# A bidirectional SSD layer: scan outputs and branch sums taken in PSUM instead of from two SBUF operands

## The chip, the cores and the metric

One core of a Trainium2 chip runs the whole layer. The metric is the device time of one execution in microseconds (us); a run of the kernel gives one number, and the median of several runs is compared. For this kernel 0.2% is about 2.6 us.

## The reference

One layer of a hybrid encoder on a sequence of 512 tokens with 1,024 features, all in 32-bit floats. What matters here is the state-space branch of the mixer:

- `h = RMSNorm(x)`, then one projection gives `z`, the scan inputs (after a short convolution and SiLU: `xs`, `B`, `C`) and two step sizes per head, `dt_fwd` and `dt_bwd`.
- 32 heads of 64 features are in 4 groups of 8 heads. Each head is scanned forward and backward in chunks of 128 tokens. In each direction the output of a token is `y_diag` (from its own chunk) plus `y_off = (C . state that enters the chunk) * exp(a_cum)`, where `a_cum` is the running sum of `dt * A` within the chunk.
- `y = y_fwd + y_bwd + d_skip * xs`, then `y * SiLU(z)` is normalised over each group of 512 features, and the normalised `y` is projected by `w_branch_ssd` (2,048 to 1,024).

Then come a windowed attention branch, a gated merge with an output projection, cross-attention into a memory of 256 tokens, a SwiGLU feed-forward part and a last RMSNorm.

## The kernel before, in words

Activations lie with features on the 128 partitions and the 512 tokens along the free dimension. Each weight is split into a high and a low half in a reduced-precision matmul format, and so is each activation; a product is three matmuls (L140 to L142), so that TensorE has 3 matmuls of 128x512 per weight block. Weights are read in pieces of 128x1024 by SyncE; ScalarE makes the high half (L130), VectorE the low half (L131).

The eight PSUM banks are three pools: three banks `mm` for projections, two `sa`, three `sb`. A bank is free for its next matmul when its last reader is done.

The scan stage runs from about 100 to 530 us. For each of the 4 groups the steps of `group_in` (projection and convolution of `B`, `C`, `xs`), `group_z` (the gate), `group_scan` and `group_out` are lists of closures which `weave` merges. Group g's `group_out` is merged into the scan of group g+1, and the last one stands alone behind the scans.

- `group_scan`, per head: SyncE loads a row of `a_cum`, spread over the partitions, into `rt` (L519); GpSimd masks it (`affine_select`, L538), ScalarE takes exponentials (L545), GpSimd adds the two directions into `mt` (L551), VectorE multiplies by `C.B` (L556), TensorE multiplies with `xs` into a bank `sa` (L566).
- Per pair of heads, `arrive` (L572) makes the arriving part of both directions in two `sb` banks, `yo[i,0]` and `yo[i,1]` (L578), and `gather` (L582) puts the output together: L586 makes `vv = xs * d_skip + yd`; L590 multiplies the loaded exponentials `ear` by `yo` and writes the product over `ear` in SBUF; L591 adds this to `vv`, on VectorE for the forward and on GpSimd for the backward direction. The forward part has tokens 128 to 511, the backward part tokens 0 to 383.
- `gate` (L595) multiplies `vv` by the gate (L603), splits it (L192, L193) and adds its square into `sq_acc` (L188).
- `group_out` (L637): eight accumulations of 12 matmuls in `mm` banks. For group 0, L645 writes `acc * vrow` into `bs`. For groups 1 to 3, L648 (VectorE) writes `acc * vrow` into the SBUF tile `cvt`, of which there is one, and L649 (GpSimd) adds it to `bs`. `vrow` is the row of norm factors. The convolution (L416 to L418) uses the same tile `cvt`.
- `apply_early` (L664) multiplies four blocks of `bs` by the merge gate once the last `group_out` has filled them.

What each engine does in which order is not written by hand alone: the kernel runs in two blocks opened with `schedule_with_timeline_sim=True` (L1136), in which a planner takes the program order as priority and a model of durations, and writes the order of each engine. The first block ends at about 530 us. At run time each engine takes its instructions strictly in that order.

Of the kernel before, what the change touches and what calls it, by code (L numbers as in the profile page):

```python
# [9 lines left out]
F32 = mybir.dt.float32  # L10
F32R = mybir.dt.float32r
AF = mybir.ActivationFunctionType
ALU = mybir.AluOpType
AX = mybir.AxisListType

P = 128
D = 1024
S = 512
# [55 lines left out]
def bidir_hybrid_layer(ctx: ExitStack, tc: tile.TileContext, io, dbg=None):  # L74
    nc = tc.nc
# [12 lines left out]
    bs = x1  # L88
# [6 lines left out]
    def bank(tag):  # L95
        return ps.tile([P, 512], F32, tag=tag, name=tag, bufs={"mm": 3, "sa": 2, "sb": 3}[tag])
# [16 lines left out]
    def gcol(c):  # L113
        return vec[:, c:c + 1]
# [20 lines left out]
    def mac(acc, w, xh, xl, nk=KT, k0=0, w0=0, first=True, last=True):  # L135
        hi, lo = w
        for k in range(nk):
            wh = hi[:, (w0 + k) * P:(w0 + k + 1) * P]
            wl = lo[:, (w0 + k) * P:(w0 + k + 1) * P]
            nc.tensor.matmul(acc, wh, xh[:, k0 + k], start=first and k == 0, stop=False)  # L140
            nc.tensor.matmul(acc, wh, xl[:, k0 + k], start=False, stop=False)  # L141
            nc.tensor.matmul(acc, wl, xh[:, k0 + k], start=False, stop=last and k == nk - 1)  # L142
# [55 lines left out]
    st = {}  # L198
# [5 lines left out]
    def full(src):  # L204
        return (src, 1024)
# [284 lines left out]
    def group_scan(g):  # L490
# [91 lines left out]
        def gather(i):  # L582
            def f():
                st["vv", i] = vv = st["sp"].tile([P, S], F32, tag="vv", name="vv", bufs=2)
                ear = st["ear", i]
                nc.vector.scalar_tensor_tensor(vv, st["xs", g, i], gcol(V_DSK + 4 * g + i), st["yd", i],  # L586
                                               op0=ALU.mult, op1=ALU.add)
                for d, eng in ((0, nc.vector), (1, nc.gpsimd)):
                    t = slice(P, S) if d == 0 else slice(0, S - P)
                    nc.vector.tensor_tensor(ear[:, d, t], ear[:, d, t], st["yo", i, d][:, t], op=ALU.mult)  # L590
                    eng.tensor_tensor(vv[:, t], vv[:, t], ear[:, d, t], op=ALU.add)  # L591
            return f


# [20 lines left out]
        for t in range(HPG + LAG3 + 1):  # L615
# [3 lines left out]
            if t >= LAG3 and (t - LAG3) % 2 == 0 and t < HPG + LAG3:  # L619
                i = (t - LAG3) // 2  # L620
                order += [nn[i], ar[i]]
            if t >= LAG3 + GLAG and (t - LAG3 - GLAG) % 2 == 0:
                i = (t - LAG3 - GLAG) // 2
# [13 lines left out]
    def group_out(g):  # L637
        def f2(q):
            def f(w):
                for j in range(2):  # L640
                    m = 2 * q + j
                    acc = bank("mm")
                    mac(acc, w, st["vh"], st["vl"], nk=4, w0=4 * j)
                    if g == 0:
                        nc.vector.tensor_tensor(bs[:, m], acc, st["vrow"], op=ALU.mult)  # L645
                    else:
                        t = st["sp"].tile([P, S], F32, tag="cvt", name="cvt", bufs=1)
                        nc.vector.tensor_tensor(t, acc, st["vrow"], op=ALU.mult)  # L648
                        nc.gpsimd.tensor_tensor(bs[:, m], bs[:, m], t, op=ALU.add)  # L649
            return f  # L650
        return [(f2(q), (full(io["w_bs"][g, q]),)) for q in range(4)]

# [589 lines left out]
```

## Time and profile before

| | |
|---|---|
| median of 3 runs | 1304.64 us (1303.63 to 1304.96) |
| the profiled execution: its time | 1304.59 us |
| the profiled execution: its span, first to last instruction | 1302.8 us |
| TensorE busy | 1253.3 us (96%) |
| VectorE, ScalarE, GpSimd busy | 770.9, 565.7, 314.8 us (59%, 43%, 24%) |
| mean granted TensorE clock | 0.989 |

How to read it: the time of an execution is its span and 1.8 us around it. PE is TensorE's matmul, PEld its weight load, DVE VectorE, ACT ScalarE, POOL GpSimd, SP SyncE. A row of the timeline has its start, its duration, and in brackets the idle time of the engine just before it with what ended that idle time. Consecutive instructions of one kind are merged (x2), and their rows can overlap by some 0.1 us, since an engine begins an instruction while the one before is still writing.

### The profile page before, as it was taken

To read this page: it belongs to the slowest core of one execution; us is meant where nothing else is said; L and a number is where in the kernel's file an instruction comes from. 1 tells how busy PE (TensorE), PEld (TensorE's weight loads), DVE (VectorE), ACT (ScalarE), POOL (GpSimd) and SP (SyncE) were. 2 spreads that over 40 slices of the span, in tenths; PEclk is the share of its full clock that TensorE was granted. 3 is DMA by queue.
4 is the path that set the end of the run, shared out by engine and by line. 5 is a ranking of instruction groups with operands and counts; after the bars stand their busy time and mean duration, and the time that the engine had idled before them with its cause. 6 is when DMAs were issued, how large, how long until landed. Compare 5 with 4: busy or idle time off the path is not lost.

```text
span 1302.8 us, 16247 instructions
## 1 busy us (share of the span) xinstructions
PE 1253.3 (96%) x6076; PEld 1015.5 (78%) x6076; DVE 770.9 (59%) x1226; ACT 565.7 (43%) x1062; POOL 314.8 (24%) x259
## 2 busy tenths in 40 slices
PE   7898999999989999999999999999999999999996
PEld 5677787778778688877667888887888888888886
DVE  6693987687787865678874345675444444432323
ACT  6456655365465232358783234444332222222220
POOL 2343742432671733211000002001111111110001
PEclk9899999999999999999999999999999999999998
DMA  7337563444354232331104233311322222233331
GB/s 267 121 112 196 158 202 113 130 146 140 105 157 133 81 116 79 120 97 33 49 29 139 95 104 108 125 65 65 97 90 98 95 96 98 95 93 101 93 98 65
DMA packets 49614, 143.48 MB, mean 110 GB/s; under 512 B 5120, under 2 KB 8576, under 8 KB 49536
## 3 DMA queue, kind: packets, MB, share of 16 engines
q1 hardware_dynamic: 47536, 138.58, 34.4%
q0 software_dynamic: 704, 2.10, 0.4%
q10 hardware_dynamic: 1296, 1.77, 0.4%
q8 instruction: 48, 0.79, 0.3%
q14 instruction: 30, 0.25, 0.1%
HBM read 137.97 MB, written 4.46 MB: 109 GB/s over the span
## 4 chain that ended last, share of the span: by engine, by line
PE 59%; issue 5%; DVE 2%; ACT 2%; POOL 1%; DVEq 0%; ACTq 0%; POOLq 0%
PE mm L140 18%; PE mm L141 18%; PE mm L142 18%; PE sb L824 1%; PE sb L811 1%; PE sb L998 1%; PE sa L967 1%; POOL rsw L723 1%; PE sa L783 1%; ACT rsw L722 0%; PE sa L785 0%; ACT whi L130 0%; ACT sm L796 0%; PE sb L155 0%; PE sb L173 0%
## 5 line engine op out<-in xcount | busy, mean ns | idle before, releaser
L130 ACT CAST whi<-raw 128x1024 fp32r<-128x1024 f32 (+2 forms) x192 | 198.8, 1036 | 457.5 <-PE mm L141 392.0
L140 PE MATMUL mm<-hh,whi 128*128 128x512 f32 x968 | 381.8, 395 | 8.1 <-ACT hh L316 4.7
L141 PE MATMUL mm<-hl,whi 128*128 128x512 f32 x968 | 381.0, 394 | 0.8 <-DVE hl L317 0.8
L142 PE MATMUL mm<-hh,wlo 128*128 128x512 f32 x968 | 381.0, 394 | 0.0
L131 DVE TENSOR_TENSOR wlo<-raw,whi 128x1024 fp32r<-128x1024 f32 (+2 forms) x193 | 238.1, 1234 | 143.6 <-ACT whi L130 134.2
L140 PEld LDWEIGHTS mm<-hh,whi 128*128 128x128 f32 x968 | 182.3, 189 | 47.9 <-ACT hh L316 4.9
L142 PEld LDWEIGHTS mm<-hh,wlo 128*128 128x128 f32 x968 | 182.6, 189 | 38.8 <-issue 2.2
L141 PEld LDWEIGHTS mm<-hl,whi 128*128 128x128 f32 x968 | 182.6, 189 | 37.6 <-issue 1.2
L545 ACT ACTIVATE rt<-rt,nb 128x128 f32<-128x128 f32 x256 | 78.6, 390 | 58.5 <-POOL rt L538 58.4
L188 POOL TENSOR_TENSOR sq_acc<-sq_acc,sq 128x512 f32<-128x512 f32 x14 | 24.4, 1741 | 261.0 <-ACT sq L187 261.0
L1051 POOL TENSOR_TENSOR fa<-fa,row 128x512 f32<-128x512 f32 x22 | 38.8, 1762 | 192.7 <-ACT fa L1050 192.7
L140 PE MATMUL mm<-vh,whi 128*128 128x512 f32 (+1 forms) x192 | 71.9, 375 | 6.9 <-DVE cvu L415 2.7
L415 DVE SCALAR_TENSOR_TENSOR cvu<-mm,hcw,cvu 128x510 f32<-128x510 f32 (+1 forms) x96 | 71.3, 743 | 7.0 <-ACT cvu L412 5.5
L140 PE MATMUL mm<-fh,whi 128*128 128x512 f32 (+1 forms) x198 | 72.7, 367 | 0.0
L141 PE MATMUL mm<-fl,whi 128*128 128x512 f32 (+1 forms) x198 | 72.4, 366 | 0.0
L142 PE MATMUL mm<-fh,wlo 128*128 128x512 f32 (+1 forms) x198 | 72.4, 366 | 0.0
L142 PE MATMUL mm<-vh,wlo 128*128 128x512 f32 (+1 forms) x192 | 71.8, 374 | 0.0
L141 PE MATMUL mm<-vl,whi 128*128 128x512 f32 (+1 forms) x192 | 70.3, 366 | 0.0
L538 POOL TENSOR_SCALAR_AFFINE_SELECT rt<-rt 128x512 f32<-128x512 f32 x64 | 49.7, 802 | 59.1 <-DMA rt<-adr 58.9
L1053 DVE TENSOR_TENSOR ft<-fa,mm 128x512 f32<-128x512 f32 x22 | 15.1, 688 | 73.6 <-PE mm L142 71.4
L551 POOL TENSOR_TENSOR mt<-rt 128x512 f32<-128x512 f32 x32 | 45.6, 1436 | 19.6 <-PE sa L566 19.5
L141 PE MATMUL mm<-ol,whi 128*128 128x512 f32 x128 | 50.0, 391 | 0.0
(231 smaller groups left out, 1963.5 us busy)
## 6 DMA issues: line engine op xcount, KB each, us to landing
raw<-in_w_in SPq DMA_DIRECT2D x69, 512.0 KB, 3.5
raw<-in_w_fi SPq DMA_DIRECT2D x44, 512.0 KB, 3.4
rt<-adr SPq DMA_DIRECT2D x32, 512.0 KB, 5.5
ear<-edr SPq DMA_DIRECT2D x32, 256.0 KB, 4.4
raw<-in_w_bs SPq DMA_DIRECT2D x16, 512.0 KB, 3.5
raw<-in_w_fo SPq DMA_DIRECT2D x16, 512.0 KB, 3.6
raw<-in_w_xk SPq DMA_DIRECT2D x8, 512.0 KB, 3.9
raw<-in_w_ba SPq DMA_DIRECT2D x8, 512.0 KB, 3.4
```

The source lines that it names most:

```text
L130: nc.scalar.copy(hi[:, t], raw[:, t])
L131: (nc.gpsimd if i in LO_POOL else nc.vector).tensor_tensor(lo[:, t], raw[:, t], hi[:, t].bitcast(F32), op=ALU.subtract)
L140: nc.tensor.matmul(acc, wh, xh[:, k0 + k], start=first and k == 0, stop=False)
L141: nc.tensor.matmul(acc, wh, xl[:, k0 + k], start=False, stop=False)
L142: nc.tensor.matmul(acc, wl, xh[:, k0 + k], start=False, stop=last and k == nk - 1)
L188: eng.tensor_tensor(acc, acc, sq, op=ALU.add)
L415: nc.vector.scalar_tensor_tensor(u[:, b], acc[:, a], w5[j], u[:, b], op0=ALU.mult, op1=ALU.add)
L538: nc.gpsimd.affine_select(out=rt[:, d].rearrange("p (c l) -> p c l", c=NCH), in_=rt[:, d].rearrange("p (c l) -> p c l", c=NCH), pattern=[[ ...
L545: nc.scalar.activation(r, r, AF.Exp, bias=st["nb"][:, c, e0:e0 + 1])
L551: nc.gpsimd.tensor_tensor(mt, st["rt", g, h][:, 0], st["rt", g, h][:, 1], op=ALU.add)
L1051: nc.gpsimd.tensor_tensor(a, a, st["row2"], op=ALU.mult)
L1053: nc.vector.tensor_tensor(t, a, st["fp", 2 * j + 1], op=ALU.mult)
```

## The change

- In `gather`, the forward product is written over `yo[i,0]` in PSUM instead of over `ear` in SBUF, and VectorE's forward addition reads it from there. The backward direction stays as it is. The order of the four instructions is the same.
- In `group_out` of groups 1 to 3, the product `acc * vrow` is written over `acc` in PSUM instead of into `cvt`, and the addition to `bs` is VectorE's and reads the product from PSUM; GpSimd's addition is gone.

```diff
@@ gather
-                for d, eng in ((0, nc.vector), (1, nc.gpsimd)):
-                    t = slice(P, S) if d == 0 else slice(0, S - P)
-                    nc.vector.tensor_tensor(ear[:, d, t], ear[:, d, t], st["yo", i, d][:, t], op=ALU.mult)
-                    eng.tensor_tensor(vv[:, t], vv[:, t], ear[:, d, t], op=ALU.add)
+                f, b = slice(P, S), slice(0, S - P)
+                yo = st["yo", i, 0]
+                nc.vector.tensor_tensor(yo[:, f], ear[:, 0, f], yo[:, f], op=ALU.mult)
+                nc.vector.tensor_tensor(vv[:, f], vv[:, f], yo[:, f], op=ALU.add)
+                nc.vector.tensor_tensor(ear[:, 1, b], ear[:, 1, b], st["yo", i, 1][:, b], op=ALU.mult)
+                nc.gpsimd.tensor_tensor(vv[:, b], vv[:, b], ear[:, 1, b], op=ALU.add)
@@ group_out
-                        t = st["sp"].tile([P, S], F32, tag="cvt", name="cvt", bufs=1)
-                        nc.vector.tensor_tensor(t, acc, st["vrow"], op=ALU.mult)
-                        nc.gpsimd.tensor_tensor(bs[:, m], bs[:, m], t, op=ALU.add)
+                        nc.vector.tensor_tensor(acc, acc, st["vrow"], op=ALU.mult)
+                        nc.vector.tensor_tensor(bs[:, m], bs[:, m], acc, op=ALU.add)
```

## Rows read from the trace of the kernel before

**Rows 1.** The page's part 1: busy us (share of the span) xinstructions.

```profile
PE 1253.3 (96%) x6076; PEld 1015.5 (78%) x6076; DVE 770.9 (59%) x1226; ACT 565.7 (43%) x1062; POOL 314.8 (24%) x259
```

**Rows 2.** The page's part 4: the chain that ended last, shares by engine.

```profile
PE 59%; issue 5%; DVE 2%; ACT 2%; POOL 1%; DVEq 0%; ACTq 0%; POOLq 0%
```

**Rows 3.** Busy time by stretch: PE, PEld, DVE, ACT, POOL, clock, DMA, GB/s.

```profile
340.00:388.00 48.00, 42.09 (x243) 34.29 (x242) 38.39 (x46) 27.56 (x72) 37.50 (x33) 1.00 0.55 154
```

**Rows 4.** Timeline of TensorE, 340 to 510 us: stalled matmuls.

```profile
347.15 0.50 PE L140 MATMUL mm<-vh,whi 128*128 128x512 f32 x1 [0.24 <-DVE cvt L648]
...
357.84 1.16 PE L449 MATMUL sb<-cf,bf 128*128 128x128 f32 x8 [1.22 <-DVE cf L418]
...
359.48 0.50 PE L140 MATMUL mm<-vh,whi 128*128 128x512 f32 x1 [0.48 <-DVE cvt L648]
...
370.42 0.47 PE L140 MATMUL mm<-vh,whi 128*128 128x512 f32 x1 [2.68 <-DVE cvu L415]
...
379.63 0.50 PE L140 MATMUL mm<-hh,whi 128*128 128x512 f32 x1 [1.29 <-DVE cvt L648]
...
509.05 0.50 PE L140 MATMUL mm<-vh,whi 128*128 128x512 f32 x1 [1.40 <-DVE cvt L648]
```

**Rows 5.** Waits of TensorE, 388 to 470 us: us in total, times, longest.

```profile
PE sa L566 <- DVE mt L556: 1.0, 2, 0.8
...
PE mm L140 <- DVE cvt L648: 0.2, 1, 0.2
```

**Rows 6.** Waits of VectorE, 340 to 388 us: us in total, times, longest.

```profile
DVE mt L556 <- POOL mt L551: 4.0, 2, 2.3
DVE cvt L648 <- POOL x L649: 2.8, 2, 1.4
DVE vv L603 <- POOL vv L591: 2.4, 2, 1.5
```

**Rows 7.** By line: duration min/median/max in ns, first and last start.

```profile
L586 DVE SCALAR_TENSOR_TENSOR vv<-xs,vec,sa x16: 732/736/748, 140.3 to 485.2; 128x512 f32<-128x512 f32 x16
...
L590 DVE TENSOR_TENSOR ear<-ear,sb x32: 536/543/554, 159.3 to 493.6; 128x384 f32<-128x384 f32 x32
...
L591 DVE TENSOR_TENSOR vv<-vv,ear x16: 542/552/1646, 160.4 to 493.1; 128x384 f32<-128x384 f32 x16
...
L603 DVE TENSOR_TENSOR vv<-vv,zs x16: 676/693/1774, 164.5 to 495.4; 128x512 f32<-128x512 f32 x16
...
L648 DVE TENSOR_TENSOR cvt<-mm,vrow x24: 674/679/694, 342.0 to 526.4; 128x512 f32<-128x512 f32 x24
```

**Rows 8.** Groups by line: busy us, mean ns of one, idle before.

```profile
L649 POOL TENSOR_TENSOR x<-x,cvt 128x512 f32<-128x512 f32 x24 | 36.5, 1522 | 17.7 <-DVE cvt L648 17.7
...
L591 DVE TENSOR_TENSOR vv<-vv,ear 128x384 f32<-128x384 f32 x16 | 10.8, 674 | 0.0
```

**Rows 9.** Timeline of VectorE, 351 to 450 us, single rows.

```profile
351.17 1.77 DVE L556 TENSOR_TENSOR mt<-mt,cb 128x512 f32<-128x512 f32 x1 [2.29 <-POOL mt L551]
...
353.86 1.76 DVE L603 TENSOR_TENSOR vv<-vv,zs 128x512 f32<-128x512 f32 x1 [0.92 <-POOL vv L591]
...
367.39 1.10 DVE L556 TENSOR_TENSOR mt<-mt,cb 128x512 f32<-128x512 f32 x1
...
377.21 1.77 DVE L556 TENSOR_TENSOR mt<-mt,cb 128x512 f32<-128x512 f32 x1
...
446.16 0.54 DVE L590 TENSOR_TENSOR ear<-ear,sb 128x384 f32<-128x384 f32 x1
...
447.79 1.65 DVE L591 TENSOR_TENSOR vv<-vv,ear 128x384 f32<-128x384 f32 x1
```

**Rows 10.** Timeline of GpSimd, 351 to 378 us, single rows.

```profile
351.09 1.30 POOL L649 TENSOR_TENSOR x<-x,cvt 128x512 f32<-128x512 f32 x1
...
352.35 1.47 POOL L591 TENSOR_TENSOR vv<-vv,ear 128x384 f32<-128x384 f32 x1
...
376.70 1.72 POOL L649 TENSOR_TENSOR x<-x,cvt 128x512 f32<-128x512 f32 x1
```

## The prediction

> **What bounds the kernel now.** I read the page's busy times first: TensorE is busy for 96% of the span, and VectorE, the next, for 59% [rows 1]. The chain that ended last says the same: it runs through TensorE, with 2% for VectorE and 1% for GpSimd [rows 2]. TensorE's work is not touched by the change, so only the moments at which TensorE stands still can move the time. Next I looked for these in the scan stage, by stretch and then in TensorE's timeline. The reader should see one bad stretch, from 340 to 388 us, where TensorE is busy for 42.1 of 48.0 us, so 5.9 us are lost, while VectorE is busy for 38.4 us and GpSimd for 37.5 us [rows 3]. Five stalls make up these 5.9 us: 0.24, 1.22, 0.48, 2.68 and 1.29 us, each ended by a VectorE instruction, three of them by L648 [rows 4]. Between 388 and 470 us, 1.0 us is lost behind L556 and 0.2 us behind L648 [rows 5], and behind the scans one stall of 1.40 us stands behind L648 [rows 4].
>
> Last I asked why VectorE is late in the bad stretch. It waits for GpSimd itself, for 4.0, 2.8 and 2.4 us, which makes 9.2 us [rows 6]. And some of its instructions are stretched. L590 and L648, which have one operand in PSUM, keep within 554 and 694 ns. L591 and L603 have the same sizes and two SBUF operands, and reach 1646 and 1774 ns [rows 7]. The stretched ones lie beside a GpSimd instruction: L556 at 351.17 us took 1.77 us while L649 ran from 351.09 [rows 9, 10].
>
> **The change part by part.** The sum is made against the profiled execution, 1304.59 us (a span of 1302.8 us and 1.8 us around it); the median of the runs, 1304.64 us, is the same to 0.1 us.
>
> *Forward gather.* 16 additions of a mean 674 ns [rows 8] become instructions with a PSUM operand, for which L590's 543 ns stands [rows 7]. VectorE saves 16 x 0.13 = 2.1 us. No row shows VectorE writing into PSUM. Below, it costs nothing more than into SBUF (L590's 536 ns); above I allow 0.06 us for each of the 40, the step from L648's 0.68 to the 0.74 us of L586, which is VectorE's dearest row of this shape that is not stretched [rows 7]. I take nothing, since the operations are L590's and L648's own; with the upper end and ten of the 40 in stalled queues it would be 0.6 us. Before 340 us this saving is covered by TensorE's own work and counts nothing; if that cover were gone it would be worth those 2.1 us at most. In exchange the `sb` bank of the forward part is held until the addition is done.
>
> *Group output.* 24 GpSimd additions of 1522 ns, 36.5 us, go [rows 8], and so does VectorE's wait for the one tile `cvt`, 2.8 us in the bad stretch [rows 6]. VectorE gets 24 additions with a PSUM operand at 0.68 us [rows 7], 16.3 us in all, and each `mm` bank comes free 0.68 us later. The bounds of one are 0.67 and 0.69 us. Queued behind each addition on VectorE are the convolution's L415, L556 and L648 of the next block, for which TensorE waits.
>
> *Stall by stall.* The stall at 347.15 us gets longer: two additions precede it where there were none, 1.4 us at most; nothing at least, if the planner puts them elsewhere; I take the middle, +0.7. The second, 1.22 us at 357.84, goes, -1.2: without L649 at 351.09, GpSimd's L591 at 352.35 starts 1.25 us earlier, and L603, which waited for it and headed the queue to L418, with it [rows 9, 10]. The third, 0.48 us, stands behind the same queue, -0.5. The fourth, 2.68 us, depends on two L556 of which one, at 367.39 us, is stretched to 1.10 us [rows 9]: between -0.4 (this one back at 0.68) and -2.7 (all of it), I take the middle, -1.6, since the queue ahead of it has also moved. The fifth, 1.29 us: L556 at 377.21 took 1.77 us beside L649 at 376.70 [rows 9, 10] and drops to 0.68, and L648's bank comes free 0.68 us later, -0.4. Bad stretch: -3.0 us. From 388 to 470 us the forward addition at 447.79 took 1.65 us [rows 9]; at 0.54 it gives back the 0.2 us behind L648 and as much of the 1.0 behind L556, -0.4. At 509.05 nothing is stretched ahead of the product, and the bank is held for one addition more, +0.7; what is late next there is nothing, as each accumulation has 12 matmuls and VectorE only two instructions. The sum is -3.0 - 0.4 + 0.7 = -2.7 us, and the time 1304.6 - 2.7 = **1301.9 us**.
>
> A rule speaks against this. VectorE's unstretched rows cost the same with a PSUM operand (L648, 674 ns at least) as with two SBUF operands (L603, 676 ns) [rows 7]. The Trainium skill (Perfetto Trace Analysis, Optimizing Scalar/DVE Operations) gives VectorE about 60 ns of access overhead on SBUF and about 125 ns on PSUM; by that the 40 instructions that turn to PSUM would cost 40 x 0.065 = 2.6 us more of VectorE, an estimate from that page, and with about ten of them in stalled queues the time would be 1302.5 us. The trace does not agree, so by its rows nothing is added.
>
> **The rivals.**
> *GpSimd was the cause of nearly all of it.* For: VectorE waits 9.2 us for GpSimd in the bad stretch [rows 6], more than the 5.9 us that TensorE loses. Against: 4.0 us of these end with L551, behind masks and exponentials that stay. All stalls of the bad stretch go, and the 1.2 us after it, with the +0.7 at the end: 1304.6 - 5.9 - 1.2 + 0.7 = 1298.2 us.
> *Nothing moves.* VectorE's 8 new additions in the bad stretch, 8 x 0.68 = 5.4 us, use up what the shorter waits and rows give it; or the planner's new order makes as many stalls as it removes. Then 1304.6 us.
> *VectorE becomes the bound of the stretch.* Place: 340 to 388 us. It is busy for 38.4 of 48 us [rows 3]; the 8 additions delay every bank release behind them. If the waits for GpSimd turn into waits for the loads or exponentials behind L551 instead, all 5.4 us reach TensorE, and 0.7 us at the end: 1304.6 + 6.1 = 1310.7 us. It decides as soon as less than 5.4 us of the 9.2 us is given back. The Trainium skill (the same page and section) has the rule that work may be moved to GpSimd when VectorE is saturated; this change does the reverse, in the one stretch where it matters, though the same place warns that the two share a read port.
> *The forward `sb` bank.* Two of three `sb` banks hold the arriving parts, and the forward one is now held until the addition, which starts 1.6 us after the product at 446.16 us [rows 9]. If one gather in four makes TensorE wait so long, 4 x 1.6 = 6.4 us come on top of the sum: 1301.9 + 6.4 = 1308.3 us. Against: TensorE's rows show no stall behind L590 now [rows 4, 5].
>
> **How the numbers follow.** My forecast has 0.40, of which 0.27 lies below 1302.0 us. A measurement of this kernel can tell 0.2% from no change, 2.6 us, so faster means below 1302.0 us and slower above 1307.2 us. GpSimd as the cause has 0.17, nothing moves 0.20, VectorE as the bound 0.15, the `sb` bank 0.08. Faster: 0.27 + 0.17 = 0.44. Same: 0.13 + 0.20 = 0.33. Slower: 0.15 + 0.08 = 0.23. The range goes from a little under the first rival's time to the `sb` bank's, 1297.5 to 1308.5 us; most of VectorE as the bound lies outside, and something below, together under 2 in 10. The forecast's own range is 1300.5 to 1304.0 us, from the ends of the first and fourth stalls.
>
> **What would show it.** Right: VectorE's forward additions all near 0.54 us, no wait of VectorE for GpSimd's sum, L603 and L556 stretched less often, and TensorE losing about 3 us instead of 5.9 between 340 and 388 us, with a longer stall, about 2.1 us, near 509 us. Wrong: new waits of TensorE's L140 behind the new addition, or of L578, L471 or L504 behind the forward addition; stalls between 159 and 340 us that moved though nothing in them was costed, which would mean the planner's order and not the durations decides; or additions out of PSUM well over 0.7 us.

## The result, and the profile after

The changed kernel takes 1312.28 us (median of 4 runs, 1310.02 to 1314.03) against 1304.80 us of the kernel before on the same chip (4 runs, 1303.63 to 1305.76): 1.0054 times as long, with a 95% interval of [1.0036, 1.0072]. It is slower, where the forecast was 1301.9 us, and 1312.28 us lies outside the range. The profiled execution took 1311.36 us, with a span of 1309.6 us: 6.8 us more than the span of before.

Busy times and the engines' shares of the chain that ended last, from the page of the changed kernel; they answer to [rows 1, 2].

```profile
PE 1254.2 (96%) x6076; PEld 1016.3 (78%) x6076; DVE 773.0 (59%) x1250; ACT 566.2 (43%) x1062; POOL 273.9 (21%) x235
...
PE 73%; issue 8%; DMA 7%; DVE 5%; POOL 3%; ACT 3%; SPq 0%; POOLq 0%; DVEq 0%; ACTq 0%
```

The work is as it was said to be: GpSimd has 24 instructions and 40.9 us less, VectorE 24 more and only 2.1 us more. TensorE's busy time is the same to 0.9 us. So the time went into moments at which TensorE stands still or runs at a lower clock. To find them I cut the span at the same three instructions in both kernels: the L173 that opens the block of the third scan, the first L504 of the last group, and the stalled L140 behind the scans. Busy time by stretch, first of before (PE, PEld, DVE, ACT, POOL, granted clock, DMA share, GB/s):

```profile
339.56:429.52 89.96, 83.43 (x440) 68.36 (x439) 70.25 (x90) 47.33 (x105) 45.97 (x40) 1.00 0.50 141
...
429.52:509.05 79.53, 76.73 (x395) 60.26 (x393) 53.91 (x66) 25.38 (x44) 36.24 (x27) 1.00 0.31 100
509.05:1302.80 793.75, 780.29 (x3662) 634.59 (x3662) 398.90 (x736) 307.23 (x542) 98.06 (x65) 0.99 0.28 89
```

and of the changed kernel, with two shorter stretches from within the first:

```profile
339.88:433.20 93.32, 84.01 (x436) 69.21 (x435) 71.01 (x97) 46.95 (x105) 31.24 (x32) 0.95 0.48 136
...
433.20:515.00 81.80, 77.59 (x398) 60.72 (x396) 55.39 (x78) 25.71 (x45) 20.70 (x19) 1.00 0.29 97
515.00:1309.60 794.60, 781.20 (x3662) 634.98 (x3662) 399.90 (x741) 307.44 (x542) 86.23 (x57) 0.99 0.28 89
...
340.00:388.00 48.00, 38.69 (x214) 31.47 (x213) 37.54 (x51) 26.32 (x70) 24.47 (x27) 0.89 0.57 154
...
370.00:380.00 10.00, 4.42 (x11) 3.49 (x12) 8.79 (x14) 6.89 (x19) 4.19 (x5) 0.50 0.35 119
```

Until the first cut 0.3 us is lost (339.88 - 339.56), in the third scan 3.4 us, in the last scan and up to the output projection 2.3 us, and behind it 0.8 us, which makes the 6.8 us. In the third scan TensorE is idle for 9.3 us instead of 6.5, all of it before 388 us, where [rows 3] had 5.9. And there is something that the profile of before had not shown in this stretch: from 370 to 380 us the granted clock is 0.50, which is 1.2 instead of 2.4 GHz. TensorE's 4.42 busy us there hold, by that clock, the work of some 2.2. Over the two scans together, up to the last cut, it is idle for 13.5 us instead of 9.3 and busy for 1.4 us more, which with the 0.3 and the 0.8 us is the 6.8 again.

Which wait ends last? TensorE's timeline of the changed kernel, stalled matmuls, and one matmul behind the long stall with one at full clock; it answers to [rows 4]. After the change L649 is the product, written in PSUM, and L650 VectorE's sum.

```profile
344.93 1.09 PE L566 MATMUL sa<-mt,xk 128*64 128x128 f32 x14 [1.48 <-DVE mt L556]
346.45 0.50 PE L140 MATMUL mm<-vh,whi 128*128 128x512 f32 x1 [0.44 <-DVE x L650]
...
347.26 0.40 PE L140 MATMUL mm<-vh,whi 128*128 128x512 f32 x1
...
375.58 0.76 PE L140 MATMUL mm<-vh,whi 128*128 128x512 f32 x1 [7.39 <-DVE x L650]
...
376.99 0.63 PE L140 MATMUL mm<-vh,whi 128*128 128x512 f32 x1
...
515.00 0.50 PE L140 MATMUL mm<-vh,whi 128*128 128x512 f32 x1 [3.19 <-DVE x L650]
```

One stall of 7.39 us, where the fourth had 2.68, makes the third scan longer, and the stall behind the scans has grown from 1.40 to 3.19 us. Behind the long one a matmul takes 0.63 us instead of 0.40, while the half clock lasts. L650 ends the long stall, but it isn't its cause. VectorE's timeline of the changed kernel, and then ScalarE's, GpSimd's and SyncE's:

```profile
364.65 1.21 DVE L131 TENSOR_TENSOR wlo<-raw,whi 128x1024 fp32r<-128x1024 f32 x1
371.18 1.53 DVE L415 SCALAR_TENSOR_TENSOR cvu<-mm,hcw,cvu 128x510 f32<-128x510 f32 x2 [5.31 <-ACT cvu L412]
372.62 0.69 DVE L649 TENSOR_TENSOR mm<-mm,vrow 128x512 f32<-128x512 f32 x1
...
374.75 0.68 DVE L650 TENSOR_TENSOR x<-x,mm 128x512 f32<-128x512 f32 x1
```

```profile
369.49 0.98 ACT L545 ACTIVATE rt<-rt,nb 128x128 f32<-128x128 f32 x3 [4.98 <-POOL rt L538]
370.38 0.76 ACT L412 ACTIVATE cvu<-mm,hcw 128x512 f32<-128x512 f32 x1
371.04 1.56 ACT L545 ACTIVATE rt<-rt,nb 128x128 f32<-128x128 f32 x5
```

```profile
361.63 2.54 POOL L551 TENSOR_TENSOR mt<-rt 128x512 f32<-128x512 f32 x2
368.82 1.22 POOL L538 TENSOR_SCALAR_AFFINE_SELECT rt<-rt 128x512 f32<-128x512 f32 x2 [4.64 <-DMA rt<-adr]
```

```profile
362.96 0.36 SPq L519 DMA_DIRECT2D rt<-adr  x1
```

Read upwards, this is the chain. GpSimd's L551 releases the buffer `rt`, SyncE issues the load of a head at 362.96 us, the mask L538 waits 4.64 us for it, and three exponentials of that head wait on ScalarE until 369.49. L412, the first instruction of the convolution of the last group's `xs`, has nothing to do with that head, but stands behind the three on ScalarE. L415 waits for L412, L649 and L650 stand behind L415 on VectorE, and TensorE needs the bank. VectorE stands idle for 5.31 us in the stretch that was feared to have too much of it.

The same instruction in the kernel before, from ScalarE's timeline:

```profile
360.58 0.76 ACT L412 ACTIVATE cvu<-mm,hcw 128x512 f32<-128x512 f32 x1
...
363.20 1.28 ACT L545 ACTIVATE rt<-rt,nb 128x128 f32<-128x128 f32 x4 [1.85 <-POOL rt L538]
```

There L412 ran at 360.58 us, ahead of the exponentials that wait. The change touches no line of ScalarE. In the changed kernel the heads of the last group on ScalarE stand as head 0, head 1, three exponentials of head 2, then L412; in the kernel before as head 0, then L412. The planner, which writes each engine's order from a model of durations, has written another one.

The end of the scans is the planner's order too. VectorE's timeline of the changed kernel:

```profile
512.47 1.90 DVE L649 TENSOR_TENSOR mm<-mm,vrow 128x512 f32<-128x512 f32 x3 [2.52 <-ACT vrow L179]
514.27 1.88 DVE L650 TENSOR_TENSOR x<-x,mm 128x512 f32<-128x512 f32 x3
```

Three products stand ahead of three sums, so that the first bank is free after four instructions and not after two.

By line, the changed kernel's durations (min/median/max in ns, first and last start), which answer to [rows 7]:

```profile
L590 DVE TENSOR_TENSOR sb<-ear,sb x16: 545/554/564, 160.8 to 495.7; 128x384 f32<-128x384 f32 x16
L591 DVE TENSOR_TENSOR vv<-vv,sb x16: 535/548/550, 161.9 to 497.3; 128x384 f32<-128x384 f32 x16
...
L649 DVE TENSOR_TENSOR mm<-mm,vrow x24: 682/688/700, 342.3 to 529.0; 128x512 f32<-128x512 f32 x24
L650 DVE TENSOR_TENSOR x<-x,mm x24: 672/680/689, 345.7 to 529.7; 128x512 f32<-128x512 f32 x24
```

### The profile page after: what moved, and what is told of

Its sections match the earlier page's. It is cut to its first block, busy times and chain, and to the rows that moved or that the text cites. A ratio compares the mean times of both kernels' runs of the same rounds, so it can differ in the third digit from the quotient of the medians.

```text
span 1309.6 us, 16245 instructions
## 1 busy us (share of the span) xinstructions
PE 1254.2 (96%) x6076; PEld 1016.3 (78%) x6076; DVE 773.0 (59%) x1250; ACT 566.2 (43%) x1062; POOL 273.9 (21%) x235
## 4 chain that ended last, share of the span: by engine, by line
PE 73%; issue 8%; DMA 7%; DVE 5%; POOL 3%; ACT 3%; SPq 0%; POOLq 0%; DVEq 0%; ACTq 0%
PE mm L140 22%; PE mm L141 21%; PE mm L142 21%; DMA rt<-adr 5%; PE sb L825 1%; PE sb L504 1%; PE sb L812 1%; POOL mt L551 1%; POOL rsw L724 1%; PE sb L578 1%; PE sb L999 1%; ACT whi L130 1%; ACT rt L545 1%; PE sa L968 1%; POOL rt L538 1%
## 5 line engine op out<-in xcount | busy, mean ns | idle before, releaser
L140 PE MATMUL mm<-hh,whi 128*128 128x512 f32 x968 | 383.0, 397 | 9.0 <-ACT hh L316 5.1
L140 PEld LDWEIGHTS mm<-hh,whi 128*128 128x128 f32 x968 | 182.7, 189 | 48.6 <-ACT hh L316 5.3
L140 PE MATMUL mm<-vh,whi 128*128 128x512 f32 (+1 forms) x192 | 71.9, 374 | 12.8 <-DVE x L650 11.0
L415 DVE SCALAR_TENSOR_TENSOR cvu<-mm,hcw,cvu 128x510 f32<-128x510 f32 (+1 forms) x96 | 71.3, 742 | 12.3 <-ACT cvu L412 10.8
L140 PE MATMUL mm<-fh,whi 128*128 128x512 f32 (+1 forms) x198 | 72.6, 367 | 0.0
L538 POOL TENSOR_SCALAR_AFFINE_SELECT rt<-rt 128x512 f32<-128x512 f32 x64 | 47.5, 766 | 69.3 <-DMA rt<-adr 69.1
L140 PEld LDWEIGHTS mm<-vh,whi 128*128 128x128 f32 x192 | 37.9, 197 | 20.3 <-ACT rt L545 7.6
L551 POOL TENSOR_TENSOR mt<-rt 128x512 f32<-128x512 f32 x32 | 45.3, 1427 | 24.8 <-PE sa L566 23.8
```

Of the source, the lines that this page charges most:

```text
L415: nc.vector.scalar_tensor_tensor(u[:, b], acc[:, a], w5[j], u[:, b], op0=ALU.mult, op1=ALU.add)
L538: nc.gpsimd.affine_select(out=rt[:, d].rearrange("p (c l) -> p c l", c=NCH), in_=rt[:, d].rearrange("p (c l) -> p c l", c=NCH), pattern=[[ ...
L551: nc.gpsimd.tensor_tensor(mt, st["rt", g, h][:, 0], st["rt", g, h][:, 1], op=ALU.add)
```

## The experiments

Two theories were set against each other. **Theory A**: the planner's order is the cause. Without GpSimd's 24 sums its model puts L412 behind exponentials whose load isn't there. **Theory B**: the change's own cost is the cause, the banks held through a second instruction and 24 more instructions on VectorE. In the table, the third scan, the stretch to the stall behind the scans and the rest are cut as above, in us of the profiled execution. "Ahead" counts ScalarE's exponentials (8 for each head) that ran ahead of the first L412 of the last group, and "L412" is when that L412 starts, in us behind the first cut. The stall is TensorE's longest between 360 and 390 us, and the end stall is the one behind the scans.

| kernel | ratio to before [95%] | third scan | to end stall | rest | ahead | L412 | stall | end stall |
|---|---|---|---|---|---|---|---|---|
| before | 1 | 90.0 | 79.5 | 793.8 | 200 | 21.0 | 2.68 | 1.40 |
| changed | 1.0054 [1.0036, 1.0072] | 93.3 | 81.8 | 794.6 | 211 | 30.5 | 7.39 | 3.19 |
| e1_gather | 1.0013 [0.9999, 1.0026] | 90.4 | 79.3 | 795.2 | 200 | 21.1 | 2.68 | 1.40 |
| e2_out | 1.0049 [1.0032, 1.0066] | 92.9 | 81.5 | 796.2 | 211 | 29.9 | 5.00 | 3.19 |
| e3_conv_first | 1.0008 [0.9991, 1.0025] | 86.8 | 81.8 | 795.8 | 200 | 23.6 | none | 3.19 |
| e4_sbuf_add | 1.0005 [0.9995, 1.0016] | 90.5 | 80.4 | 794.9 | 208 | 25.9 | 5.45 | 1.40 |
| e5_order_back | 0.9988 [0.9977, 0.9998] | 87.2 | 80.9 | 793.2 | 200 | 20.7 | 1.34 | 3.19 |
| e6_order_and_tile | 0.9969 [0.9952, 0.9986] | 86.9 | 79.1 | 794.6 | 200 | 20.7 | 1.11 | 1.40 |
| e7_before_late | 1.0083 [1.0066, 1.0100] | 99.3 | 80.0 | 795.3 | 211 | 33.2 | 11.15 | 1.40 |
| e8_tile_only | 1.0029 [1.0014, 1.0043] | 93.3 | 80.1 | 793.2 | 211 | 29.9 | 7.56 | 1.40 |
| e9_idle_sums | 1.0025 [1.0012, 1.0038] | 89.4 | 81.8 | 795.3 | 208 | 25.5 | 2.56 | 3.19 |
| e10_no_gather | 0.9966 [0.9952, 0.9980] | 87.0 | 79.1 | 793.4 | 200 | 21.1 | 1.17 | 1.40 |
| e11_other_edge | 0.9975 [0.9960, 0.9990] | 88.1 | 80.0 | 793.3 | 200 | 23.6 | 0.77 | 1.40 |
| e12_both_again | 0.9957 [0.9941, 0.9973] | 86.7 | 79.1 | 793.4 | 200 | 20.7 | 0.54 | 1.40 |

The start of L412 is counted from the first cut because the third scan itself starts between 337.8 and 345.4 us.

Two things can be read from the columns before any single run. Among the kernels with the changed work, the third scan goes with the place of L412: with 200 exponentials ahead it takes 86.7 to 88.1 us, with 208 it takes 89.4 and 90.5, with 211 it takes 92.9 and 93.3. Among those with the group output of before (before, e1_gather, e7_before_late) it takes 90.0 and 90.4 us with 200 and 99.3 with 211. And the two scans together account for most of the ratios: against before's 169.5 us they are 5.6 us longer in the changed kernel (by its ratio 7), 9.9 in e7_before_late (11), 3.9 in e8_tile_only (4), and 3.7 us shorter in e12_both_again (6).

**The two parts alone.** The gather's part of the diff without the rest:

> The first part alone (forward product and sum through PSUM); the group output as before. Theory A (the planner's new order on ScalarE, set off by taking GpSimd's 24 sums away, puts a convolution's first instruction behind exponentials whose load has not landed): this kernel keeps ScalarE's order of before, so 1303 to 1306 us, no stall over 3 us. Rival B (banks held longer by the in-place product and sum, here the forward sb bank): 1306 us or more, with TensorE waiting behind the forward sum.

and the group output's part without the rest:

> The second part alone (group output in PSUM, its sum on VectorE); the gather as before. Theory A: ScalarE has the changed kernel's order, so the whole loss: 1310 to 1314 us, one stall of about 7 us near 370 us followed by half clock. Rival B: it holds the mm banks, so the same 1310 or more, but with several stalls of about 1 us spread over the group outputs.

The gather alone takes 1307.26 us (10 runs) against 1306.16 (25 runs of before), 1.0013 [0.9999, 1.0026]. The number lies in the range of Rival B, but the kernel before was at 1306 us on this chip too, and TensorE waits nowhere behind the forward sum. L412 has its place of before. Four of the five stalls of the bad stretch are those of before (0.23, 1.28, 0.48 and 2.68 us), and the fifth, 1.29 us, is gone; but from 369.6 to 372.7 us the granted clock is 0.50, and the third scan takes 90.4 us. The output alone takes 1312.35 us (4 runs), 1.0049 [1.0032, 1.0066]: all that the whole change lost, within the intervals. It has the long stall too, with 5.00 us instead of the expected 7, and no new stalls of about 1 us spread over the group outputs, as Rival B wanted them. TensorE's timeline of e2_out, and a stretch by busy time:

```profile
374.17 0.77 PE L140 MATMUL mm<-vh,whi 128*128 128x512 f32 x1 [5.00 <-DVE x L648]
...
513.73 0.80 PE L140 MATMUL mm<-vh,whi 128*128 128x512 f32 x1 [3.19 <-DVE x L648]
```

```profile
511.00:519.00 8.00, 5.27 (x12) 4.14 (x13) 5.48 (x9) 0.29 (x2) 0.00 (x0) 0.63 0.01 4
```

In this execution the stall behind the scans is followed by half clock as well; in the changed kernel's profiled execution it wasn't.

**Some exponentials held behind L412.** The changed kernel, with the exponentials of the third group's head 7 issued behind L412, which stand ahead of it in the changed kernel too:

```diff
-        nc.scalar.activation(u, acc, AF.Identity, ...)
+        st["l412"] = nc.scalar.activation(u, acc, AF.Identity, ...)
...
+                with tc.issue_after(st["l412"].ins) if g == 2 and h == 7 else ExitStack():
                     ... nc.scalar.activation(r, r, AF.Exp, ...)
```

> The changed kernel with one edge more: the exponentials of head 7 of the third group are issued behind the first convolution instruction of the next group's first x block. All work and all bank holding stay. Theory A: the 7.4 us stall goes, with its clock drop: 1303.5 to 1307 us. Rival B (bank holding and 24 more instructions on VectorE): nothing changes, 1310 to 1314 us.

It took 1307.05 us (10 runs), 1.0008 [0.9991, 1.0025]. The loss is gone to within 0.25%. By the clock of the whole execution L412 seems late, at 368.99 us, but the third scan of this execution begins late: counted from there it starts after 23.6 us, where the changed kernel had 30.5 and the kernel before 21.0. Heads 0 and 1 of the last group stand ahead of it, but head 7 of the third group no longer does, so that 200 exponentials ran ahead of it, as many as before. TensorE has no stall above 1.5 us in the whole bad stretch, and the third scan takes 86.8 us. The profiled execution was one of the longer ones, 1311.63 us, and of the 7.0 us that its span has more than that of before, 5.9 lie ahead of the first cut (345.44 against 339.56 us). Up to there TensorE has the same 1582 matmuls in both; it is idle for 3.2 us more, 2.6 of them in the first 60 us, and busy for 2.7 us more, with the granted clock at 0.94 from 140 to 200 us, where before it was 1.00.

**The sum from SBUF.** The whole change, but with the product of `group_out` written into the SBUF tile `cvt` as before, so that the bank is free after one instruction; the sum stays VectorE's:

```diff
-                        nc.vector.tensor_tensor(acc, acc, st["vrow"], op=ALU.mult)
-                        nc.vector.tensor_tensor(bs[:, m], bs[:, m], acc, op=ALU.add)
+                        t = st["sp"].tile([P, S], F32, tag="cvt", name="cvt", bufs=1)
+                        nc.vector.tensor_tensor(t, acc, st["vrow"], op=ALU.mult)
+                        nc.vector.tensor_tensor(bs[:, m], bs[:, m], t, op=ALU.add)
```

> The changed kernel, but the group output's product goes to the one SBUF tile again and VectorE adds from there: the mm bank is free as early as in the kernel before, VectorE has the same 24 sums more, with two SBUF operands. ScalarE's order has 16 exponentials ahead of the same convolution instruction. Theory A: the long stall stays, 3 us or more near 370 us, 1308 to 1315 us. Rival B: with the banks free early the loss goes, 1303 to 1306 us.

TensorE's timeline of e4_sbuf_add:

```profile
371.19 0.76 PE L140 MATMUL mm<-vh,whi 128*128 128x512 f32 x1 [5.45 <-DVE cvu L415]
...
510.93 0.50 PE L140 MATMUL mm<-vh,whi 128*128 128x512 f32 x1 [1.40 <-DVE cvt L650]
```

Theory A had the stall right and the time wrong. L412 stood behind heads 0 and 1 of the last group, and the stall of over 3 us stayed; but the kernel took 1306.68 us (10 runs), 1.0005 [0.9995, 1.0016], which lies between the two ranges and nearer to Rival B's. Part of it is the place of L412, which is not the changed kernel's: three exponentials fewer stand ahead of it, and it starts 25.9 us behind the cut instead of 30.5. The stall behind the scans is back at 1.40 us. So the bank's second instruction costs something where a bank is waited for, and Theory A alone isn't enough.

**L412 put back in its place.** The changed kernel, with the exponentials of the last group's heads 1 to 7 issued behind that group's L412, which is where L412 stands among the exponentials in the kernel before; no work is changed:

```diff
+                with tc.issue_after(st["l412", 12].ins) if g == 3 and h > 0 else ExitStack():
                     ... nc.scalar.activation(r, r, AF.Exp, ...)
```

> The changed kernel with one edge more: the exponentials of heads 1 to 7 of the last group are issued behind the first convolution instruction of that group's first x block, as the planner had it in the kernel before. Work and bank holding are those of the changed kernel. Theory A (the order on ScalarE): the stall of 7.4 us is gone and 4 to 6 us of the 7 come back, ratio 0.999 to 1.002; what remains is the stall near 510 us, 3.2 us instead of 1.4, with a clock drop in some executions. Rival B (longer bank holding and 24 more VectorE instructions): ratio stays at 1.004 or more.

It took 1305.13 us (12 runs) against 1308.01 (29 runs of before), 0.9988 [0.9977, 0.9998]: 1.0054 has become a little faster than before. TensorE's timeline of e5_order_back, ScalarE's, and the bad stretch by busy time (L651 is the sum, L546 the exponentials):

```profile
369.81 0.47 PE L140 MATMUL mm<-vh,whi 128*128 128x512 f32 x1 [1.34 <-DVE x L651]
...
508.68 0.50 PE L140 MATMUL mm<-vh,whi 128*128 128x512 f32 x1 [3.19 <-DVE x L651]
```

```profile
361.32 0.77 ACT L412 ACTIVATE cvu<-mm,hcw 128x512 f32<-128x512 f32 x1
...
370.11 1.28 ACT L546 ACTIVATE rt<-rt,nb 128x128 f32<-128x128 f32 x4 [5.68 <-POOL rt L538]
```

```profile
340.00:388.00 48.00, 44.74 (x248) 36.49 (x247) 39.36 (x54) 26.98 (x66) 18.55 (x21) 1.00 0.50 144
```

ScalarE waits for the late load no less, 5.68 us where the changed kernel's ScalarE waited 4.98, but now nothing that TensorE needs stands behind it. The stall is 1.34 us, the clock stays at 1.00, and TensorE loses 3.3 us (48.00 - 44.74) in the bad stretch, where the forecast had about 3. The end stall is still 3.19 us.

**Both mended.** e5_order_back, with the product of the last group alone in the tile (`if g == 3` around the edit of e4_sbuf_add), to bring the end stall back to 1.40 us:

> As the run before, and in the last group alone the product goes to the SBUF tile, so that its mm bank is free after the product; VectorE adds from there. Theory A: the stall near 510 us is 1.4 us again and its clock drop goes, so 2 to 4 us less than the run before, ratio 0.996 to 0.999, faster than both kernels. Rival B: ratio 1.002 or more, since groups 1 and 2 still hold their banks.

1304.63 us (12 runs), 0.9969 [0.9952, 0.9986], with the end stall at 1.40 us. The same kernel was run again later, against 30 runs of before with a median of 1307.35 us:

> The run with both repairs once more, beside the two above on one chip. Theory A: ratio 0.996 to 0.999 again. If its gain was this chip's spread: 0.999 to 1.001.

1302.61 us (8 runs), 0.9957 [0.9941, 0.9973]. This version is faster than the kernel before in both runs, by 0.3 and 0.4%, and by these ratios faster than the changed kernel too.

**The other way round.** If the place of L412 is the cause, the kernel before must become slower by that place alone. No line of the change is in it; L412 of the last group waits in ScalarE's order for heads 0 and 1 and the first three exponentials of head 2:

```diff
+                        if g == 3 and (h < 2 or h == 2 and 4 * d + c < 3):
+                            tc.add_manual_dep(st["l412", 12].ins, ex.ins.name, ...NoSync..., reason="late")
```

> The kernel before with one order changed: the first convolution instruction of the last group's first x block is issued behind the exponentials of that group's heads 0, 1 and three of head 2, as in the changed kernel. No work differs from the kernel before. Theory A: TensorE stalls for 5 us or more near 370 us, 3 to 5 us longer in all, ratio 1.002 to 1.004. Rival B: no difference, ratio 0.999 to 1.001.

1318.21 us (6 runs), 1.0083 [1.0066, 1.0100]: slower by more than the change itself, and by more than was expected. TensorE's timeline of e7_before_late, and ScalarE's:

```profile
381.84 0.77 PE L140 MATMUL mm<-vh,whi 128*128 128x512 f32 x1 [11.15 <-DVE cvu L415]
```

```profile
373.15 0.98 ACT L545 ACTIVATE rt<-rt,nb 128x128 f32<-128x128 f32 x3 [3.30 <-POOL rt L538]
374.04 0.76 ACT L412 ACTIVATE cvu<-mm,hcw 128x512 f32<-128x512 f32 x1
```

L412 comes 3.7 us later than in the changed kernel (374.04 against 370.38; 2.7 us, counted from the first cut), and the stall is 11.15 us. GpSimd's timeline of e7_before_late has the reason (L555 is L551 of before):

```profile
365.18 2.53 POOL L555 TENSOR_TENSOR mt<-rt 128x512 f32<-128x512 f32 x2
...
372.08 2.87 POOL L538 TENSOR_SCALAR_AFFINE_SELECT rt<-rt 128x512 f32<-128x512 f32 x4 [2.66 <-DMA rt<-adr]
```

The instruction that releases the buffer `rt` runs at 365.18 us and not at 361.63, and the load for which L412 has to wait is issued 3.5 us later, at 366.49 instead of 362.96. The rest lies behind L412: from its start to the end of the stall 7.8 us pass instead of 5.2. VectorE's L415 stand there among instructions with two SBUF operands, of which one took 1.74 us. The direction was right, the size too small.

**The end stall alone.** The changed kernel with the last group's product in the tile, L412 left where the planner puts it:

> The changed kernel with the last group's product in the SBUF tile, its sum on VectorE; nothing else, so ScalarE keeps the changed kernel's order. Both theories agree on the end: the stall near 510 us is 1.4 us again. Theory A: the long stall near 370 us stays, so 1.5 to 4 us less than the changed kernel, ratio 1.002 to 1.004. Rival B: the last group was a third of the held banks, so a third of the loss goes, ratio 1.003 to 1.004, and no stall longer than 3 us.

1311.37 us (12 runs), 1.0029 [1.0014, 1.0043]. The end stall is 1.40 us, the other one 7.56 us where Rival B wanted none over 3, and the kernel is still slower than before. Its interval overlaps the changed kernel's, so what the tile gives by itself isn't settled by this run. With the place of L412 alone undone (e5_order_back) the kernel wasn't slower than before any more; with the end stall alone undone it was.

With the changed kernel, e5_order_back and e6_order_and_tile this run makes a square: the place of L412 mended or not, the tile there or not. The place is worth 6.1 us of the third scan without the tile (93.3 to 87.2) and 6.4 with it (93.3 to 86.9), and another 0.9 us of the next stretch both times. The tile is worth 1.7 us of that stretch in the planner's order (81.8 to 80.1), 1.8 in the mended one (80.9 to 79.1), and 0.0 and 0.3 us of the third scan. The ratios say the same: 0.0066 and 0.0060 for the place, 0.0025 and 0.0019 for the tile.

**Sums that nobody needs.** The changed kernel, and behind each of VectorE's 24 sums one of GpSimd of the old size, into a tile that isn't read:

```diff
+                        t = st["sp"].tile([P, S], F32, tag="cvt", name="cvt", bufs=1)
+                        nc.gpsimd.tensor_tensor(t, bs[:, m], st["vrow"], op=ALU.add)
```

> The changed kernel with 24 sums on GpSimd that nobody needs (bs + vrow into the SBUF tile), behind VectorE's sums; the output is the same. With them the planner puts the first convolution instruction of the last group's x0 behind heads 0 and 1, no longer behind three exponentials of head 2 too. Theory A (order, set off by GpSimd's missing sums): in spite of 24 instructions more it is faster than the changed kernel, ratio 1.000 to 1.003, and the stall near 370 us is shorter than 7 us. Rival B (bank holding, VectorE's load): VectorE's two-operand instructions are stretched again on top of the held banks, so slower than the changed kernel, ratio 1.006 or more.

1310.31 us (12 runs), 1.0025 [1.0012, 1.0038]. The kernel has 24 instructions more than the changed one and isn't slower than it: 1.0025 against 1.0054, with intervals that just touch. The planner puts L412 behind heads 0 and 1 only, and the stall is 2.56 us. The third scan takes 89.4 us, no longer than before's 90.0; what the profiled execution has more lies ahead of the first cut (3.2 us), up to the end stall, which stays at 3.19 us (2.3), and behind it (1.6). That speaks for the place of L412 and against VectorE's load, which is that of the changed kernel. It doesn't show that the missing sums moved L412: the idle sums also use the tile `cvt` again, and e4_sbuf_add, which uses the tile with no sum on GpSimd, has L412 in the same place.

**What the gather's part is worth, and another order.** e6_order_and_tile with the gather of the kernel before:

> The run with both repairs (order and last group's tile), but with the gather of the kernel before: what the forward part through PSUM is worth by itself. Its forward sums have two SBUF operands again, up to 1.6 us each beside a GpSimd instruction. If it is worth anything: 1 to 2 us slower than with it, ratio 0.998 to 0.999. If VectorE's time there is covered by TensorE: the same ratio, 0.996 to 0.998.

1302.81 us (11 runs), 0.9966 [0.9952, 0.9980], beside 0.9957 [0.9941, 0.9973] with the new gather: the two can't be told apart. And e3_conv_first with the last group's product in the tile:

> The changed kernel with the last group's product in the SBUF tile, and the order mended by the other edge (head 7 of the third group behind the convolution instruction). Theory A: the long stall is gone as with the first edge, ratio 0.996 to 0.999. Rival B: 1.003 or more, as with the tile alone.

1304.36 us (12 runs), 0.9975 [0.9960, 0.9990], with the end stall at 1.40 us. Two different orders, each with the tile, are both faster than before.

## Why the prediction was wrong

**The step that failed** is the one that went stall by stall through the order of before. It took that order as fixed and asked only how long each instruction would be. The fourth stall, -1.6 us with bounds of -0.4 and -2.7, became +4.7 (7.39 against 2.68), with half clock behind it: over the two scans TensorE is busy for 1.4 us more. Not a duration moved it: L412 changed its place on an engine that the diff doesn't touch. The prediction names the planner three times, as the lower end of the first stall, as a rival in which new stalls make up for old ones, at 1304.6 us, and as a sign of being wrong, but it gave it no case on the slower side. e5_order_back and e7_before_late show what the place does with the same work, in both directions: 1.0054 to 0.9988 in the changed kernel, 1 to 1.0083 in the one before.

**The bounds of a step that hangs on the order.** -0.4 to -2.7 came from the durations of two L556, of which only the one at 367.39 us was taken as stretched; the other, at 365.05 us, took 1.76 us. What a reordering could cost was in the profile before too. From SyncE's timeline and GpSimd's:

```profile
365.04 1.62 SPq L519 DMA_DIRECT2D rt<-adr  x2
```

```profile
370.61 3.87 POOL L538 TENSOR_SCALAR_AFFINE_SELECT rt<-rt 128x512 f32<-128x512 f32 x4 [2.67 <-DMA rt<-adr]
```

A head's load took 5.6 us there from the issue to the mask, and 5.9 in the changed kernel (362.96 to 368.82); an instruction that is put behind such a mask can be late by as much. None of the prediction's waits was read on ScalarE.

**The first stall**, taken as +0.7 and at most 1.4, was +1.7: 1.48 and 0.44 us stand where 0.24 did. Two products stand together ahead of the sums on VectorE, from 342.34 us, and the planner let TensorE's L566, which waits for L556, go ahead of the L140 that had filled this time before. The same two stalls are in e5_order_back, so this term was under-sized in the good order also.

**The second, third and fifth stalls** are gone, as taken (-1.2 and -0.5) or better than taken (-1.3 instead of -0.4). The fifth is gone in e1_gather too, where GpSimd still has its sums, so the reason that was given for it isn't shown. In e5_order_back the bad stretch loses 3.3 us instead of 5.9, -2.6 where the sum had -3.0, and its third scan is 2.8 us shorter than that of before. With L412 in its old place the mechanism of the forecast holds in the bad stretch, and its size too.

**From 388 to 470 us**, -0.4 was -0.8: the stalls there are 1.0 us instead of 1.8. The 1.8 include 0.6 us behind L418 at 399.36 us, which the prediction didn't count and which is gone. In e5_order_back the stalls there are 2.4 us, so in the good order this term isn't borne out.

**The end**, +0.7, was +1.8. Not one addition more is waited for, but two products and one addition: three products stand ahead of the first sum. "What is late next there is nothing" was right for the matmuls and left out the clock, which was half behind this stall in e2_out.

**The durations** were right. L649 and L590, which now write into PSUM, have medians of 688 and 554 ns where writing in SBUF had 679 and 543 [rows 7]; that is some 10 ns for each of the 40, and the upper bound of 0.06 us was not needed. The forward additions keep within 550 ns, where before they reached 1646. The Trainium skill's larger PSUM overhead (Perfetto Trace Analysis, Optimizing Scalar/DVE Operations), which was weighed against the rows, isn't seen: the sums with one PSUM operand have a median of 680 ns, where L603 with two SBUF operands had 676 at the least and 693 in the median [rows 7]. The instructions beside GpSimd are stretched less, as expected; groups by line of the changed kernel (busy, mean ns | idle before):

```profile
L605 DVE TENSOR_TENSOR vv<-vv,zs 128x512 f32<-128x512 f32 x16 | 13.5, 846 | 7.2 <-POOL vv L593 7.2
```

L605 is L603 of before, whose mean in the same view was 1093 ns. That the gather's part is worth little was right as well: neither e1_gather nor e10_no_gather can be told from the kernel that it differs from by the gather alone.

**The signs and the ranges.** One sign of being wrong was a stall between 159 and 340 us that moved: the one behind L418 near 190 us went from 1.00 to 2.06 us, though up to the first cut only 0.3 us were lost in all. The forecast's own range doesn't follow from its ends: +-0.7 of the first stall and -1.1 to +1.2 of the fourth give 1300.1 to 1303.8 us, and not 1300.5 to 1304.0. Neither bears on the step that failed.

**The rivals.** "VectorE becomes the bound of the stretch" came nearest in its time, 1310.7 us, and was wrong in its mechanism: VectorE was idle for 5.31 us just where it would have had to be the bound, and e5_order_back has the same additions without the loss. The nearness is luck. The `sb` bank held longer shows in none of the stalls. "Nothing moves" named the planner's new order, but as one that makes up for what it takes; here it took more.

What stays open: what led the planner to move L412, GpSimd's missing sums or the tile `cvt` that the group output no longer takes, since the kernels that bring the tile back in the third scan have L412 in the same place with the sums and without them. And the terms of the square (some 7 us for the place, some 2 for the tile) are those of whole kernels, in each of which the planner may have changed other places too.

## What to carry to other kernels

Where a planner writes each engine's order, a change of work is also a change of order on engines that it doesn't touch, so compare first which instruction stands behind which wait on every engine, and then the durations. A release that TensorE needs should not stand behind a wait for a load on any engine on its way; here one ordering edge and one SBUF tile turned 0.5% slower into 0.3 to 0.4% faster. And a bank that is multiplied in place and then added is held until the second instruction, which may stand behind other products.

## What was not expected of the hardware

- A stall can cost more than its length. Within the 7.39 us in which TensorE stood still (up to 375.58 us) the granted clock fell: it was 0.50 from 370 to 380 us, and a matmul took 0.63 us instead of 0.40. Around the end stall of 3.19 us it was 0.63 on average from 511 to 519 us in e2_out, and 1.00 in the profiled execution of the changed kernel. Behind the stall of 2.68 us it was 0.50 from 369.6 to 372.7 us in e1_gather, and 1.00 in the kernel before. So a stall of one length doesn't always bring it.
- On VectorE, multiplying a PSUM bank in place costs no more than 10 ns over writing the product in SBUF (688 against 679 ns for 128x512).
- Executions of one program differed by more than the three runs of before had let expect: e3_conv_first took 1301.54 to 1312.58 us in 10 runs, against 1303.63 to 1304.96 in those three. The longer executions had the lower mean granted clock: 0.982 in the longest of these ten, 0.991 in the shortest. A difference of 0.2% needed ten runs and more on each side.
